# Four weight buffers shared across stages, odd Fourier weights made in place, and a Nyquist row summed by VectorE

## The chip, the core and the metric

The kernel runs on one core of one Trainium2 chip. The core has TensorE (PE in the profile) for matmuls, VectorE (DVE), ScalarE (ACT) and GpSimd (POOL) for the rest, and SyncE (SP), which here only issues transfers. Each engine takes its instructions in order and waits for others by semaphores. Transfers (DMAs) are issued by SP, ACT and POOL. The metric is the time of the whole program on the device in microseconds (us).

## The reference

Two layers of an encoder over 512 tokens with 1024 channels, in float32. Each layer is a half-step feed-forward network (FFN), a gated pair of mixers, and a second half-step FFN:

```python
x += 1/2 * SwiGLU(RMSNorm(x))                       # FFN 1, width 2816
x += W_o( g_na * NA(h) W_na + g_f * FNet(h) W_f )   # mixer, h = RMSNorm(x)
x += 1/2 * SwiGLU(RMSNorm(x))                       # FFN 2
...
s = einsum(q, k_window) * scale + bias              # neighbourhood attention, 8 heads
p = softmax(s);  o = einsum(p, v_window)
f = jnp.fft.fft2(ug, axes=(1, 3), norm="ortho").real   # Fourier mixer, 4 groups of 128
```

The gates g_na and g_f are sigmoids of `h @ w + gate_bias`. A last RMSNorm follows the second layer.

## The kernel before, in words

**Weights as a stream.** All weights lie in DRAM as granules of 128x1024 floats, 512 KB each. `stage_items` lists the granules in the order of their use, and `Stream` (`ws`) works through the list. `fetch` loads (L155, by SP) up to `depth` = `FETCH` = 8 items ahead of the one that is prepared next, and never beyond the current `stage`; `ws.enter(stage)` opens the next one. `prep` makes two tiles from a granule: `whi`, a rounded copy by ScalarE (L207, or L202 with the sign changed), and `wlo`, what the rounding lost, by VectorE (L210, L203). Three buffers of each exist. TensorE multiplies with both and with the rounded and lost parts of the activations: twelve matmuls of 512 columns for one granule (L534, L535, L537).

**Sums of weights.** The large products are done with seven products of half-size blocks in place of eight (Strassen's scheme), for which weights have to be added. Blocks are called a, b, c, d, and products m1 to m7. Where a tile needs the sum of two granules, either GpSimd issues a second transfer that adds in memory (L165 after the load, L212 after the granule has been used once), or VectorE adds two tiles (L179). In the first gate block, the products run in the order 1, 2, 5, 6, 7, 3, 4; m7 uses c (with a added by L165), m3 uses d with first a and then b added (L212).

**Buffers.** In an FFN stage the granules lie in nine buffers `raw` of the stage's own pool, which `swap_pools` opens and closes. In the mixer they lie in slots of a general pool (`slot`, 23 buffers), which also holds activations. The attention's bias tiles `bm` (one per head, 512 KB) have four buffers in the mixer's stage pool; `bias_for` loads two of them by SP.

**End of the mixer, start of the gates.** The order of DVE, ACT and PE is written out by hand here; SP and POOL are ordered by the scheduler. Attention probabilities of pairs 5, 6 and 7 are made (`maxes` on DVE with the bias tiles, L1433; exponentials on ACT; transposes and products on PE), in between the Fourier part. `part_f` multiplies with four Fourier weights. For each of the two column halves i there are two granules t1 and t2; the kernel uses t1 + t2 ("even") and t1 - t2 ("odd"). The even one is loaded with t2 added by GpSimd. For the odd one t1 is loaded a second time beside t2, and DVE subtracts (L179). `f_both` forms sum and difference in `fs` and `gs`, and `f_turn` copies rows of `gs` in mirrored places of `fs` by 8 small transfers for each i (L1681, "flips"). The Nyquist row (one frequency that stands alone) is the sum of three rows that `last_f` leaves on partitions 0, 32 and 64 of a PSUM bank; `f_last` copies the bank (L1686) and adds the rows by three tiny GpSimd transfers into row 3 of `fs` (L1691, L1693). `minus` makes the differences of activations for the gates' products in two steps (L1623). Then `gate_block` runs twice: at m7 the result of earlier products is copied out by ScalarE (`snap`, tile `sn`, L619) before TensorE writes to the same bank again.

Of the kernel before, what the change touches and what calls it, by code (L numbers as in the profile page):

```python
# [18 lines left out]
P = 128  # L19
# [15 lines left out]
FETCH = 8  # L35
# [63 lines left out]
def encoder_kernel(  # L99
# [8 lines left out]
    wp = ctx.enter_context(tc.tile_pool(name="wp", bufs=1))  # L108
    kp = ctx.enter_context(tc.tile_pool(name="kp", bufs=1))
# [9 lines left out]
    def slot(dt=F32, s="k", shape=(4, 256)):  # L119
        return kp.tile([P, *shape], dt, tag="k", name=nm(s), bufs=23)  # L120

# [23 lines left out]

    class Raw:
        def __init__(self, key, n=1024, plus=None):
            self.key, self.n, self.plus, self.t = key, n, plus, None

        def load(self, parts=1):  # L150
            if self.t is None:
                self.t = raw_pool[0](self.n)
                for c in range(0, self.n, self.n // parts):
                    cs = slice(c, c + self.n // parts)
                    nc.sync.dma_start(out=self.t[:, cs], in_=wst[GRAN_AT[self.key]][:, cs])  # L155
# [11 lines left out]
    class Item:  # L167
        def __init__(self, raw, add=None, neg=False, stage=0, parts=1, pieces=1, then=None, op=ALU.add):
            self.raw, self.add, self.neg, self.stage, self.parts, self.op = raw, add, neg, stage, parts, op
            self.pieces, self.then = pieces, then  # L170

# [5 lines left out]
        def summed(self):  # L177
            if self.add:
                V.tensor_tensor(self.raw.t, self.raw.t, self.add.t, self.op)  # L179
                self.add = None  # L180

        def prep_high(self):

            self.summed()
            n, t = self.raw.n, self.raw.t
            hi, lo = [wp.tile([P, 1024], F32R, tag=s, name=nm(s), bufs=3)[:, 0:n] for s in ("whi", "wlo")]
            S.activation(hi, t, AF.Copy)
            self.out = (hi, lo)

            def low():  # L190
                self.last = V.tensor_tensor(lo, t, hi.bitcast(F32), ALU.subtract)

            return low

        def prep(self, nxt):
# [8 lines left out]
            else:  # L204
                for c in range(0, n, n // self.parts):
                    cs = slice(c, c + n // self.parts)
                    S.activation(hi[:, cs], t[:, cs], AF.Copy)  # L207
                    if nxt:
                        nxt.summed()
                    self.last = V.tensor_tensor(lo[:, cs], t[:, cs], hi[:, cs].bitcast(F32), ALU.subtract)  # L210
            if self.then:
                G.dma_start(out=t, in_=wst[GRAN_AT[self.then]][:, 0:n], accum_op=ALU.add)  # L212
            self.out = (hi, lo)
# [3 lines left out]
    def stage_items():  # L217
# [52 lines left out]
        for l in range(L):  # L270
# [9 lines left out]
            for t1, t2 in halves:  # L280
                add(Raw(t1, plus=t2))
            for t1, t2 in halves:
                add(Raw(t1), Raw(t2), op=ALU.subtract)
# [840 lines left out]
    def stage_mixer(l, norm, nxt):  # L1124
# [94 lines left out]
        def proj_UV():  # L1219
# [31 lines left out]
            bias_for(0)  # L1251
# [4 lines left out]
            k0 = proj_T(None)  # L1256
            step(7)
# [94 lines left out]
        def four_high(ps, z):  # L1352
# [7 lines left out]
            def low_of():  # L1360
# [6 lines left out]
                V.tensor_copy(nyq[:, z, 0:1], ps[:, 256:257])  # L1367
# [4 lines left out]
        def four_ends(ps):  # L1372
# [7 lines left out]
            def low_of():  # L1380
                V.scalar_tensor_tensor(e_, g.bitcast(F32), ch[:, 162:163], t, ALU.mult, ALU.add)
                V.tensor_tensor(nyq[:, 2, 0:1], ps[:, 256:257], ch[:, 160:161], ALU.mult)
# [5 lines left out]
        def bias_for(hp):  # L1388
            bms[hp] = []
            for e in range(2):  # L1390
                res = mp.tile([P, 4, 256], F32, tag="bm", name=nm("bm"), bufs=4)
                nc.sync.dma_start(out=res, in_=bias_in[(l * NH + 2 * hp + e)])
# [290 lines left out]
        def f_last(i, ps):  # L1683

            t = tmp(s="fl")
            V.tensor_copy(t[0:96], ps[0:96])  # L1686
            to = fs[i, 0][3:4, 1, :]
            for z in range(3):
                row = t[32 * z : 32 * z + 1]
                if z == 0:  # L1690
                    G.dma_start(out=to, in_=row)  # L1691
                else:
                    G.dma_start(out=to, in_=row, accum_op=ALU.add)  # L1693

        with tc.manual_schedule(engines={mybir.EngineType.DVE, mybir.EngineType.Activation}):
            with tc.manual_schedule(engines={mybir.EngineType.PE}):
# [90 lines left out]
                p[5].maxes(1)  # L1787
                p[5].exps(0)
# [5 lines left out]
                pf = [part_f(0, t, f_w[0], 0) for t in range(2)]  # L1794
                att_split(po[0])
# [13 lines left out]
                att_split(po[1])  # L1809
                p[6].maxes(0)  # L1810
# [11 lines left out]
                pl = [last_f(i, raws[i]) for i in range(2)]  # L1822
                p[7].maxes(0)
                p[7].maxes(1)
                p[6].scaled(0)
# [5 lines left out]
                for i in range(2):  # L1831
                    f_last(i, pl[i])
# [3 lines left out]
                p[7].inverse(1)  # L1836
                p[7].scaled(0)
                p[7].scaled(1)
                first = minus(B[0, 0], B[0, 1], "t1")
                next(first)  # L1840
                next(first)
                pt_[6] = kept(ts)
                att_split(po[2])
                ws.enter(ws.stage + 1)
# [5 lines left out]
                swap_pools(0)  # L1850
# [141 lines left out]
    def swap_pools(kind, fetch=True):  # L1992
# [219 lines left out]
```

## Time and profile before

| | before |
|---|---|
| median of 3 runs | 1862.14 us (1859.94 to 1864.39) |
| profiled execution | 1860.03 us |
| its span | 1858.3 us |
| mean granted TensorE clock | 0.994 |
| read from memory, written | 372.76 MB, 2.11 MB |
| weight loads of 512 KB by SP, by GpSimd | 472, 180 |

The profile shows one execution. "Busy" is the time in which an engine worked; a timeline row has start, length, engine, line, operation, tiles (out<-in) and in brackets the idle time ahead of it with the one who ended it. "SPq" is SP's own queue of instructions, which issue transfers. The clock is a share of full speed. These two lines of the page show the clock and the transfers in 40 equal slices of the span (tenths, and GB/s):

```profile
PEclk9999999999999999999999999999999999999999
GB/s 304 223 242 213 187 280 285 205 199 85 283 217 183 167 229 241 215 198 279 249 190 214 226 224 202 282 251 226 160 124 273 214 181 177 219 232 215 200 286 157
```

The tenth and the thirtieth slices, with 85 and 124 GB/s, are the ends of the two mixers.

### The profile page before, as it was taken

To read this page: it belongs to the slowest core of one execution; us is meant where nothing else is said; L and a number is where in the kernel's file an instruction comes from. 1 tells how busy PE (TensorE), PEld (TensorE's weight loads), DVE (VectorE), ACT (ScalarE), POOL (GpSimd) and SP (SyncE) were. 2 spreads that over 40 slices of the span, in tenths; PEclk is the share of its full clock that TensorE was granted. 3 is DMA by queue.
4 is the path that set the end of the run, shared out by engine and by line. 5 is a ranking of instruction groups with operands and counts; after the bars stand their busy time and mean duration, and the time that the engine had idled before them with its cause. 6 is when DMAs were issued, how large, how long until landed. Compare 5 with 4: busy or idle time off the path is not lost.

```text
span 1858.3 us, 24537 instructions
## 1 busy us (share of the span) xinstructions
PE 1829.5 (98%) x8778; PEld 1514.2 (81%) x8778; DVE 1604.3 (86%) x1938; ACT 1306.1 (70%) x1775; POOL 187.7 (10%) x231
## 2 busy tenths in 40 slices
PE   9999999999899999999999999999998899999998
PEld 7888888887778888888888888888877788888886
DVE  7878899777889987889998888997788799888899
ACT  6777875677576777787667778666675677677865
POOL 0001010110111010001010100101011101110010
PEclk9999999999999999999999999999999999999999
DMA  9898799862987788869878986978539877888695
GB/s 304 223 242 213 187 280 285 205 199 85 283 217 183 167 229 241 215 198 279 249 190 214 226 224 202 282 251 226 160 124 273 214 181 177 219 232 215 200 286 157
DMA packets 206770, 405.87 MB, mean 218 GB/s; under 512 B 109116, under 2 KB 109276, under 8 KB 206648
## 3 DMA queue, kind: packets, MB, share of 16 engines
q1 hardware_dynamic: 176536, 302.61, 50.5%
q0 software_dynamic: 29680, 101.14, 29.9%
q8 instruction: 69, 1.13, 0.3%
q10 hardware_dynamic: 432, 0.55, 0.1%
q14 instruction: 53, 0.43, 0.1%
HBM read 372.76 MB, written 2.11 MB: 202 GB/s over the span
## 4 chain that ended last, share of the span: by engine, by line
PE 90%; DMA 4%; DVE 3%; ACT 2%; issue 1%; SPq 0%; ACTq 0%; DVEq 0%
PE A L534 10%; PE A L537 10%; PE A L535 10%; PE o L537 7%; PE o L534 7%; PE o L535 7%; PE B L534 5%; PE B L535 5%; PE B L537 5%; DMA raw<-in_wst_dram 2%; PE C L534 2%; PE C L535 2%; PE C L537 2%; PE ps L339 2%; PE ps L340 2%; PE ps L341 2%
## 5 line engine op out<-in xcount | busy, mean ns | idle before, releaser
L210 DVE TENSOR_TENSOR wlo<-raw,whi 128x1024 fp32r<-128x1024 f32 (+1 forms) x534 | 632.6, 1196 | 181.0 <-ACT whi L207 177.5
L207 ACT ACTIVATE whi<-raw 128x1024 fp32r<-128x1024 f32 (+1 forms) x534 | 546.7, 1033 | 292.4 <-PE A L535 60.4
L165 POOL DMA_DIRECT2D raw<-in_wst_dram x170 | 148.9, 895 | 1218.4 <-DMA raw<-in_wst_dram 636.3
L179 DVE TENSOR_TENSOR raw<-raw,raw 128x1024 f32<-128x1024 f32 (+1 forms) x152 | 181.6, 1197 | 2.0
L535 PE MATMUL A<-whi,xl 128*128 128x512 f32 x400 | 155.7, 389 | 0.0
L534 PE MATMUL A<-whi,xh 128*128 128x512 f32 x400 | 155.7, 389 | 0.0
L202 ACT ACTIVATE whi<-raw 128x1024 fp32r<-128x1024 f32 (+1 forms) x83 | 85.7, 1037 | 46.9 <-PE A L535 11.4
L389 ACT ACTIVATE at<-zt 128x1024 uint16<-128x1024 uint16 (+2 forms) x96 | 110.3, 1166 | 11.3 <-DMA zt<-zs 11.3
L537 PE MATMUL A<-wlo,xh 128*128 128x512 f32 x400 | 115.0, 389 | 0.0
L203 DVE SCALAR_TENSOR_TENSOR wlo<-raw,whi 128x1024 fp32r<-128x1024 f32 (+1 forms) x83 | 98.8, 1198 | 12.3 <-ACT whi L202 12.3
L537 PEld LDWEIGHTS A<-wlo,xh 128*128 128x128 f32 x400 | 75.1, 188 | 15.6
L534 PEld LDWEIGHTS A<-whi,xh 128*128 128x128 f32 x400 | 75.1, 188 | 15.4
L535 PEld LDWEIGHTS A<-whi,xl 128*128 128x128 f32 x400 | 75.1, 188 | 15.4
L534 PE MATMUL B<-whi,xh 128*128 128x512 f32 x208 | 81.2, 390 | 0.0
L535 PE MATMUL B<-whi,xl 128*128 128x512 f32 x208 | 81.0, 389 | 0.0
L535 PE MATMUL C<-whi,xl 128*128 128x512 f32 x208 | 81.0, 389 | 0.0
L534 PE MATMUL C<-whi,xh 128*128 128x512 f32 x208 | 80.9, 389 | 0.0
L370 ACT ACTIVATE zs<-th 128x1024 uint16<-128x1024 uint16 x80 | 79.4, 1040 | 0.4 <-DVE th L794 0.4
L787 ACT ACTIVATE th<-sn,rh 128x512 f32<-128x512 f32 x80 | 54.8, 715 | 31.2 <-DVE sn L624 30.3
L619 ACT ACTIVATE sn<-A 128x512 f32<-128x512 f32 x104 | 58.4, 584 | 22.9 <-PE A L537 22.9
L537 PE MATMUL C<-wlo,xh 128*128 128x512 f32 x208 | 59.8, 389 | 0.0
L537 PE MATMUL B<-wlo,xh 128*128 128x512 f32 x208 | 59.8, 389 | 0.0
(446 smaller groups left out, 4641.4 us busy)
## 6 DMA issues: line engine op xcount, KB each, us to landing
raw<-in_wst_dram SPq DMA_DIRECT2D x472, 512.0 KB, 6.0
raw<-in_wst_dram POOLq DMA_DIRECT2D x180, 512.0 KB, 8.1
bm<-in_bias_dram SPq DMA_DIRECT2D x16, 512.0 KB, 5.9
raw<-in_wst_dram SPq DMA_DIRECT2D x30, 256.0 KB, 5.9
vs<-v SPq DMA_DIRECT2D x24, 128.0 KB, 5.6
x<-in_xin_dram SPq DMA_DIRECT2D x4, 512.0 KB, 10.2
raw<-in_wst_dram POOLq DMA_DIRECT2D x8, 256.0 KB, 7.4
dft<-in_dft_dram POOLq DMA_DIRECT2D x8, 256.0 KB, 6.7
```

What stands on the lines that cost most here:

```text
L165: G.dma_start(out=self.t, in_=wst[GRAN_AT[self.plus]][:, 0 : self.n], accum_op=ALU.add)
L179: V.tensor_tensor(self.raw.t, self.raw.t, self.add.t, self.op)
L202: S.activation(hi, t, AF.Copy, scale=-1.0)
L203: self.last = V.scalar_tensor_tensor(lo, t, -1.0, hi.bitcast(F32), ALU.mult, ALU.subtract)
L207: S.activation(hi[:, cs], t[:, cs], AF.Copy)
L210: self.last = V.tensor_tensor(lo[:, cs], t[:, cs], hi[:, cs].bitcast(F32), ALU.subtract)
L370: S.activation(s[:, h], words[:, h], AF.Copy)
L389: S.activation(to[:, w], t[:, w], AF.Copy)
L534: PE.matmul(ps, lh, rh, start=start, stop=False, skip_group_check=again)
L535: PE.matmul(ps, ll, rh, start=False, stop=False, skip_group_check=again)
L537: PE.matmul(ps, lh, rl, start=False, stop=stop, skip_group_check=again)
L619: S.activation(t[:, b, :], ps[b], AF.Copy)
```

## The change

1. A pool `rp` with four buffers `kr` lives through the whole program. They hold the attention's bias tiles in the mixer, then the first four granules of the gates (`mix_raw`), and FFN granules. The FFN stage's own `raw` buffers go from nine to five; `ffn_raw` takes, of all nine, the one whose last use is the oldest.
2. At the end of the mixer the stream enters the gates' stage earlier, with a depth of 6, so that the gates' first granules may be loaded there. The depth goes back to 8 afterwards.
3. The odd Fourier weight is made in the buffer of the even one: (t1 + t2) - 2 t2, by one scalar_tensor_tensor of DVE. t1 is not loaded again.
4. The Nyquist row is summed by DVE: one copy of 32x512 out of PSUM and two additions; the column that carries it is number 3, so that it comes out on the right row. `last_f(0)` runs earlier, and `f_last(0)` and `f_last(1)` stand in two places.
5. `minus` for the first difference, and the first bias load (now issued by ACT), move.

```diff
+    rp = ctx.enter_context(tc.tile_pool(name="rp", bufs=1, reuse_waits="tile"))
...
+    def kept_raw(s, shape=(1024,)):
+        return rp.tile([P, *shape], F32, tag="kr", name=nm(s), bufs=4)
...
             self.key, self.n, self.plus, self.t = key, n, plus, None
+            self.refs = self.used = 0
+
+        def use(self):
+            uses[0] += 1
+            self.refs, self.used = self.refs - 1, uses[0]
...
-                self.t = raw_pool[0](self.n)
+                self.t = raw_pool[0](self)
...
+        def __init__(self, raw, add=None, neg=False, stage=0, parts=1, pieces=1, then=None, twice=False):
+            self.raw, self.add, self.neg, self.stage, self.parts, self.twice = raw, add, neg, stage, parts, twice
             self.pieces, self.then = pieces, then
+            raw.refs += 1
+            if add:
+                add.refs += 1
...
         def summed(self):
             if self.add:
-                V.tensor_tensor(self.raw.t, self.raw.t, self.add.t, self.op)
+                if self.twice:
+                    V.scalar_tensor_tensor(self.raw.t, self.add.t, -2.0, self.raw.t, ALU.mult, ALU.add)
+                else:
+                    V.tensor_tensor(self.raw.t, self.raw.t, self.add.t, ALU.add)
+                self.add.use()
                 self.add = None
...
-                    if nxt:
+                    if nxt and not nxt.twice:
                         nxt.summed()
...
+            self.raw.use()
...
             halves = [((s, "f", 2 * i), (s, "f", 2 * i + 1)) for i in range(2)]
-            for t1, t2 in halves:
-                add(Raw(t1, plus=t2))
-            for t1, t2 in halves:
-                add(Raw(t1), Raw(t2), op=ALU.subtract)
+            even = [Raw(t1, plus=t2) for t1, t2 in halves]
+            for raw in even:
+                add(raw)
+            for raw, (_, t2) in zip(even, halves):
+                add(raw, Raw(t2), twice=True)
...
-            bias_for(0)
...
             k0 = proj_T(None)
+            bias_for(0, S)
...
-                V.tensor_copy(nyq[:, z, 0:1], ps[:, 256:257])
...
-                V.tensor_tensor(nyq[:, 2, 0:1], ps[:, 256:257], ch[:, 160:161], ALU.mult)
+                V.tensor_tensor(nyq[:, 2, 3:4], ps[:, 256:257], ch[:, 160:161], ALU.mult)
...
-        def bias_for(hp):
+        def bias_for(hp, by=nc.sync):
             bms[hp] = []
             for e in range(2):
-                res = mp.tile([P, 4, 256], F32, tag="bm", name=nm("bm"), bufs=4)
-                nc.sync.dma_start(out=res, in_=bias_in[(l * NH + 2 * hp + e)])
+                res = kept_raw("bm", (4, 256))
+                by.dma_start(out=res, in_=bias_in[(l * NH + 2 * hp + e)])
                 bms[hp].append(res)
...
         def f_last(i, ps):
 
-            t = tmp(s="fl")
-            V.tensor_copy(t[0:96], ps[0:96])
-            to = fs[i, 0][3:4, 1, :]
-            for z in range(3):
-                row = t[32 * z : 32 * z + 1]
-                if z == 0:
-                    G.dma_start(out=to, in_=row)
-                else:
-                    G.dma_start(out=to, in_=row, accum_op=ALU.add)
+            to = fs[i, 0][0:32, 1, :]
+            V.tensor_copy(to, ps[0:32])
+            for z in (1, 2):
+                V.tensor_tensor(to, to, ps[32 * z : 32 * z + 32], ALU.add)
...
                 p[5].maxes(1)
+                first = minus(B[0, 0], B[0, 1], "t1")
+                next(first)
+                next(first)
...
                 pf = [part_f(0, t, f_w[0], 0) for t in range(2)]
+                pl = [last_f(0, raws[0])]
...
                 att_split(po[1])
+                f_last(0, pl[0])
                 p[6].maxes(0)
...
                 pf = [part_f(0, t, f_w[1], 1) for t in range(2)]
-                pl = [last_f(i, raws[i]) for i in range(2)]
+                pl.append(last_f(1, raws[1]))
+                ws.enter(ws.stage + 1)
                 p[7].maxes(0)
                 p[7].maxes(1)
+                ws.items[ws.prepped].summed()
+                ws.depth = 6
+                ws.enter(ws.stage + 1)
...
                 f_copy(1, 0, pf[0])
                 f_copy(1, 1, pf[1])
-                for i in range(2):
-                    f_last(i, pl[i])
                 po.append(att_pv(2))
                 ts = transposed(p[6].s)
                 p[7].inverse(0)
                 p[7].inverse(1)
+                ws.prep(ws.pos + 2)
+                f_last(1, pl[1])
                 p[7].scaled(0)
                 p[7].scaled(1)
...
-                first = minus(B[0, 0], B[0, 1], "t1")
-                next(first)
-                next(first)
                 pt_[6] = kept(ts)
                 att_split(po[2])
-                ws.enter(ws.stage + 1)
                 ws.prep(ws.pos + 2)
                 f_w.append(ws.next(0))
                 f_both(0, 0, part_f(1, 0, f_w[2]))
...
                 ts = transposed(p[7].s)
-                swap_pools(0)
+                swap_pools(0, False)
+                ws.depth = FETCH
+                ws.enter(ws.stage)
...
-    def ffn_raw(n):
-        return scope_pool[0].tile([P, 1024], F32, tag="raw", name=nm("raw"), bufs=9)[:, 0:n]
-
-    def mix_raw(n):
+    live = {"kr": [None] * 4, "raw": [None] * 5}
+
+    def oldest(tag):
+
+        ages = [0 if r is None else (r.used if not r.refs else 1 << 30) for r in live[tag]]
+        k = min(range(len(ages)), key=lambda i: ages[i])
+        return ages[k], tag, k
+
+    def ffn_raw(raw):
+        _, tag, k = min(oldest("kr"), oldest("raw"))
+        live[tag][k] = raw
+        if tag == "kr":
+            return kept_raw("raw")[:, 0 : raw.n]
+        return scope_pool[0].tile([P, 1024], F32, tag="raw", name=nm("raw"), bufs=5)[:, 0 : raw.n]
+
+    def mix_raw(raw):
+        if raw.key[1] in ("ga", "gb") and None in live["kr"]:
+            live["kr"][live["kr"].index(None)] = raw
+            return kept_raw("raw")
         return slot(F32, "raw", (1024,))
...
             raw_pool[0] = mix_raw
+            live["kr"] = [None] * 4
         else:
             raw_pool[0] = ffn_raw
+            live["raw"] = [None] * 5
```

What the change moves, by the built programs' order. SP's queue at the end of the first layer's mixer, before: two loads `raw` (the n granules), three flips, then the six loads for a, b and d.

```order
L1211 DMA vs_724_3716<-v_709_3660 64x512 x4
L155 DMA raw_811_4166<-in_wst_dram 128x1024
L155 DMA raw_812_4168<-in_wst_dram 128x1024
L1681 DMA fs_773_3978<-gs_816_4181 60x512 x2
L1681 DMA fs_772_3976<-gs_816_4181 60x512
L155 DMA raw_821_4207<-in_wst_dram 128x1024
L155 DMA raw_822_4209<-in_wst_dram 128x1024
```

The same place in the change (raw_802 and raw_803 are a0 and a1, raw_800 and raw_801 the n granules, raw_804 and raw_820 b, raw_821 and raw_822 d):

```order
L166 DMA raw_802_4111<-in_wst_dram 128x1024
L166 DMA raw_803_4113<-in_wst_dram 128x1024
L166 DMA raw_800_4102<-in_wst_dram 128x1024
L166 DMA raw_801_4104<-in_wst_dram 128x1024
L166 DMA raw_804_4115<-in_wst_dram 128x1024
L166 DMA raw_820_4208<-in_wst_dram 128x1024
L166 DMA raw_821_4210<-in_wst_dram 128x1024
L166 DMA raw_822_4213<-in_wst_dram 128x1024
L1702 DMA fs_774_3985<-gs_815_4182 60x512 x2
L1702 DMA fs_773_3983<-gs_815_4182 60x512 x2
```

All loads now stand ahead of all flips. SP's queue at the end of the flips, before (gb: the gate biases; raw_855 and raw_858: c0 and c1):

```order
L1681 DMA fs_801_4111<-gs_835_4263 4x512 x2
L1681 DMA fs_800_4109<-gs_835_4263 3x512
L1892 DMA gb_851_4369<-in_gbias_dram 128x1024
L1892 DMA gb_852_4371<-in_gbias_dram 128x1024
L155 DMA raw_855_4375<-in_wst_dram 128x1024
L155 DMA raw_858_4382<-in_wst_dram 128x1024
```

and in the change (raw_851 and raw_854 are c0 and c1):

```order
L1702 DMA fs_806_4127<-gs_831_4258 4x512 x2
L1702 DMA fs_805_4125<-gs_831_4258 3x512
L166 DMA raw_851_4370<-in_wst_dram 128x1024
L166 DMA raw_854_4377<-in_wst_dram 128x1024
L166 DMA raw_866_4438<-in_wst_dram 128x1024
L1915 DMA gb_847_4364<-in_gbias_dram 128x1024
L1915 DMA gb_848_4366<-in_gbias_dram 128x1024
```

c0 and c1 have gone ahead of the gate biases. VectorE behind the last maxima (L1433, L1454), before: the Fourier copies, the two copies for the Nyquist rows, and the two differences.

```order
L1668 COPY fs_4109<-ps_4071 128x512
L1668 COPY fs_4111<-ps_4080 128x512
L1686 COPY fl_4113<-ps_4089 96x512
L1686 COPY fl_4118<-ps_4093 96x512
L1445 RECIPROCAL rs_4068<-sm_4067 128x2 x2
L1623 TENSOR_TENSOR t_807_4156<-xh_2214 128x1024
L1623 TENSOR_TENSOR t_808_4157<-xl_2215 128x1024
L1494 TENSOR_TENSOR o_4163<-ps_4123,o_4163 128x512
L210 TENSOR_TENSOR wlo_4171<-raw_3464,whi_4170 128x1024
```

and in the change:

```order
L194 SCALAR_TENSOR_TENSOR raw_3382<-raw_3465,raw_3382 128x1024
L1689 COPY fs_4125<-ps_4080 128x512
L1689 COPY fs_4127<-ps_4089 128x512
L1466 RECIPROCAL rs_4077<-sm_4076 128x2 x2
L229 TENSOR_TENSOR wlo_4159<-raw_3382,whi_4158 128x1024
L1707 COPY fs_4125<-ps_4098 32x512
L1709 TENSOR_TENSOR fs_4125<-fs_4125,ps_4098 32x512 x2
L1515 TENSOR_TENSOR o_4172<-ps_4129,o_4172 128x512
```

The odd weight's subtraction has come here, the differences have gone to an earlier place, and three small instructions stand for one copy (the other three stand ahead of the sixth maxima). SP's queue in the first block of the second layer's first FFN, in the change (loads are numbered in the order of the list):

```order
L166 DMA raw_1579_8224<-in_wst_dram 128x1024
L166 DMA raw_1585_8250<-in_wst_dram 128x1024
L166 DMA raw_1595_8306<-in_wst_dram 128x1024
L166 DMA raw_1604_8350<-in_wst_dram 128x1024
L166 DMA raw_1626_8479<-in_wst_dram 128x1024
L166 DMA raw_1592_8286<-in_wst_dram 128x1024
L166 DMA raw_1640_8562<-in_wst_dram 128x1024
```

Before, all loads of this stretch stood in the order of the list; now raw_1592, the third granule of c, stands behind three that are used after it. It is the granule whose buffer, counted in weight preparations along the engines' orders, is released three preparations ahead of its own; in the first block of the FFNs ahead of and behind this one (the second of each layer) it is five. Before the change it was eight or more for every granule that is added to.

More of the change, by code (lines that the diff above doesn't have):

```diff
@@ L143, in encoder_kernel @@
         PE.matmul(pw, warm[:, 0:P], warm, start=True, stop=True)
+    uses = [0]
     class Raw:
@@ L167, in encoder_kernel @@
     class Item:
-        def __init__(self, raw, add=None, neg=False, stage=0, parts=1, pieces=1, then=None, op=ALU.add):
-            self.raw, self.add, self.neg, self.stage, self.parts, self.op = raw, add, neg, stage, parts, op
+        def __init__(self, raw, add=None, neg=False, stage=0, parts=1, pieces=1, then=None, twice=False):
+            self.raw, self.add, self.neg, self.stage, self.parts, self.twice = raw, add, neg, stage, parts, twice
             self.pieces, self.then = pieces, then
+            raw.refs += 1
+            if add:
+                add.refs += 1
         def load(self):
@@ L212, in prep @@
                 G.dma_start(out=t, in_=wst[GRAN_AT[self.then]][:, 0:n], accum_op=ALU.add)
+            self.raw.use()
             self.out = (hi, lo)
@@ L1366, in low_of @@
                 V.memset(y[:, 2:4, 0:1].bitcast(F32), 0.0)
-                V.tensor_copy(nyq[:, z, 0:1], ps[:, 256:257])
+                V.tensor_copy(nyq[:, z, 3:4], ps[:, 256:257])
                 return y
```

## The prediction

> **What bounds the kernel now.** I read the page first, then the waits of TensorE, then the rows of TensorE around its waits, then the chain of work that ends in the longest of them.
>
> ```profile
> PE 1829.5 (98%) x8778; PEld 1514.2 (81%) x8778; DVE 1604.3 (86%) x1938; ACT 1306.1 (70%) x1775; POOL 187.7 (10%) x231
> engine line waited for: us in total, times, longest us
> PE A L534 <- ACT sn L619: 19.1, 4, 6.1
> PE ps L143 <- DVE ones L139: 1.2, 1, 1.2
> PE ps L340 <- DVE wlo L210: 0.4, 2, 0.2
> ```
>
> TensorE is busy for 1829.5 of 1858.3 us. Nothing that leaves its work alone can win more than the 28.8 us in which it is idle and whatever it loses to a lower clock. Two thirds of the idle time, 19.1 us, are four waits of one kind. All stand at product 7 of the gate blocks, two in each layer.
>
> ```profile
> 496.73 0.79 PE L534 MATMUL A<-whi,t3h 128*128 128x512 f32 x1 [6.13 <-ACT sn L619]
> 502.04 0.39 PE L534 MATMUL A<-whi,t3h 128*128 128x512 f32 x1
> 541.17 0.50 PE L534 MATMUL A<-whi,t3h 128*128 128x512 f32 x1 [2.67 <-ACT sn L619]
> 1417.03 0.79 PE L534 MATMUL A<-whi,t3h 128*128 128x512 f32 x1 [5.59 <-ACT sn L619]
> 1420.35 0.39 PE L535 MATMUL A<-whi,t3l 128*128 128x512 f32 x1
> 1462.63 0.80 PE L534 MATMUL A<-whi,t3h 128*128 128x512 f32 x1 [4.69 <-ACT sn L619]
> 1468.40 0.39 PE L534 MATMUL A<-whi,t3h 128*128 128x512 f32 x1
> 1468.62 0.39 PE L535 MATMUL A<-whi,t3l 128*128 128x512 f32 x1
> ```
>
> In brackets stands the wait and who ended it. At full clock these matmuls start 0.227 us apart (1468.40 to 1468.62, rounded), and one granule of weights feeds twelve, 2.72 us. After the wait of 6.13 us twelve matmuls take 502.04 - 496.73 = 5.31 us, so the slow clock costs 2.59 us more. After 5.59 us seven take 3.32 us in place of 1.59, which is 1.73 us more. After 2.67 us nothing is lost behind the wait. The first block's waits thus cost 6.13 + 2.59 + 5.59 + 1.73 = **16.0 us** in both layers. The second block's (2.67, and 4.69 with its ramp) are some 10 us, and have another cause, below.
>
> The chain of waits into 496.73 (start, us, what) says what the first kind is:
>
> ```profile
> 469.45 6.68 DMA fs<-gs
> ...
> 476.15 7.03 DMA raw<-in_wst_dram
> ...
> 483.46 11.57 DMA raw<-in_wst_dram
> ...
> 496.10 0.59 ACT sn L619
> ```
>
> The second granule c1 of product 7 is loaded at 476.15, its other half added by a GpSimd transfer at 483.46, which lands at 495.03. ScalarE, in order, converts it and then takes the snapshot `sn` that TensorE waits for. From landing to matmul it is 1.70 us. The load is late for its place in SP's in-order queue:
>
> ```profile
> 444.03 0.80 SPq L155 DMA_DIRECT2D raw<-in_wst_dram  x2
> 453.64 2.79 SPq L1681 DMA_DIRECT2D fs<-gs  x3
> 456.53 3.86 SPq L155 DMA_DIRECT2D raw<-in_wst_dram  x6
> 460.43 13.61 SPq L1681 DMA_DIRECT2D fs<-gs  x13
> 474.14 0.83 SPq L1892 DMA_DIRECT2D gb<-in_gbias_dram  x2
> 475.02 22.78 SPq L155 DMA_DIRECT2D raw<-in_wst_dram  x9
> ```
>
> Six weight loads, sixteen flips of the Fourier result and two gate biases stand ahead of it. The windows (stretch, length, busy PE, PEld, DVE, ACT, POOL, granted clock, DMA share, GB/s) show the contrast:
>
> ```profile
> 420.00:428.00 8.00, 8.00 (x49) 6.26 (x49) 4.70 (x21) 5.53 (x14) 0.00 (x0) 1.00 0.00 0
> 436.00:444.00 8.00, 8.00 (x76) 6.57 (x72) 7.05 (x19) 6.00 (x16) 0.00 (x0) 1.00 0.01 2
> 472.00:488.00 16.00, 16.00 (x73) 13.24 (x72) 15.46 (x16) 7.46 (x10) 3.28 (x4) 1.00 1.02 320
> 488.00:504.00 16.00, 9.87 (x33) 7.41 (x32) 8.53 (x8) 7.09 (x8) 1.90 (x3) 0.79 1.05 264
> ```
>
> The transfers rest until 444 and are full from 472 to 504.
>
> **The change part by part.** *Early gate weights.* The first four granules a0, a1, b0, b1 go into kept buffers. SP's new order has them ahead of the flips, and c0, c1 ahead of the gate biases; the last bias buffers are released by the score maxima. a0 and a1 fall into the empty stretch before 444. Ahead of c1 the queue no longer has the 3.86 us of six loads between flips and the 0.83 us of two biases: 4.7 us. With every transfer as long as before, c1 lands at 495.03 - 4.7 = 490.3, and TensorE starts at 492.0. It is due at 496.73 - 6.13 = 490.6, so 1.4 us of wait are left. If the accumulate takes less time in the emptier queues, nothing is left:
>
> ```profile
> raw<-in_wst_dram SPq DMA_DIRECT2D x472, 512.0 KB, 6.0
> raw<-in_wst_dram POOLq DMA_DIRECT2D x180, 512.0 KB, 8.1
> ```
>
> Its median is 8.1 us against the 11.57 here. What is late next is product 3, whose granules are added to by L212 while product 7 runs:
>
> ```profile
> L212 POOL DMA_DIRECT2D raw<-in_wst_dram x2: 863/863/863, 485.5 to 487.3; - x2
> ...
> DMA to landing us min/median/max: 12.1/13.1/14.0
> ```
>
> They land at 485.5 + 12.1 = 497.6 and 487.3 + 14.0 = 501.3. Without the wait TensorE ends product 7 at 490.6 + 24 x 0.227 = 496.05. With 1.1 us of conversion (the whi group's mean is 1.03) the first is ready at 498.7, 2.7 us late. The second, ready at 502.4, is due at 498.7 + 2.7 = 501.4, 1.0 late. So with unchanged transfers 3.7 us come back per layer, and with a median transfer of 8.1 us (landing at 493.6 and 495.4) none. Between 0 and 3.7 I take 1.5 us, next to the sum for c1 at old durations; waits under 2.67 us cost no clock. Two layers: **-16.0 + 3.0 us**.
>
> *Odd Fourier weights and the Nyquist row.* Two 512 KB loads a layer go. The subtraction on VectorE becomes a scalar_tensor_tensor of the same shape. The group means 1197 and 1198 ns say that this costs nothing:
>
> ```profile
> L179 DVE TENSOR_TENSOR raw<-raw,raw 128x1024 f32<-128x1024 f32 (+1 forms) x152 | 181.6, 1197 | 2.0
> L203 DVE SCALAR_TENSOR_TENSOR wlo<-raw,whi 128x1024 fp32r<-128x1024 f32 (+1 forms) x83 | 98.8, 1198 | 12.3 <-ACT whi L202 12.3
> 445.93 1.28 DVE L1686 COPY fl<-ps 96x512 f32<-96x512 f32 x2
> 447.89 1.21 DVE L1623 TENSOR_TENSOR t<-xh 128x1024 f32<-128x1024 f32 x1
> 452.94 0.68 DVE L1675 TENSOR_TENSOR gs<-fs,ps 128x512 f32<-128x512 f32 x1
> 453.07 0.50 PE L340 MATMUL ps<-wlo,y 128*128 128x512 f32 x1 [0.20 <-DVE wlo L210]
> ```
>
> The Nyquist row was two copies (1.28 us together) and six tiny DMAs per layer. It becomes two copies of 32x512 and four additions, which no row shows. They have 512 columns, like the copy at 0.64 and the sum from PSUM at 0.68 us; I take 0.64, six times, 3.8 us, which is 2.6 more. If fewer partitions were faster it would be less, down to nothing. Three of the six (1.9 us) stand ahead of the sixth maxima, from which one weight subtraction (1.2 us) goes, so these come 0.7 us later. The two differences of L1623 (1.21 us each) leave the stretch 447 to 450 for one where DVE is busy for 4.70 of 8 us. The wait of 0.20 us at 453.07 shows that TensorE has no reserve there, so 0.7 us come through, at most the 1.9 of three operations. I take 1.0 us a layer: **+2.0 us**. The tiny DMAs waited beside GpSimd's other work and paid nothing.
>
> *The four shared buffers in the FFN.* Nine buffers become four kept and five of the stage, chosen by the oldest use. The transfers stay as many, the order of loads on SP changes. TensorE does not wait in any FFN before. I take 0; the bound is a rival below. *First attention bias* issued by ScalarE behind a snapshot near 350 us, while the first maxima stand at 372.6 and a bias lands in about 6: 0.
>
> *Second gate block.* Its waits end with the same snapshot, but there the chain comes from a transpose:
>
> ```profile
> 529.80 9.51 DMA zt<-zs
> ...
> 539.34 0.03 ACT mq L389
> ```
>
> ScalarE, in order, stands before the words `mq` that it unpacks until the transpose lands, and the snapshot is behind it. No part of the change touches what starts this transpose, and the transfers beside it stay, so I take 0; bounds are the whole 10 us and, the other way, one 5 us load that now meets it.
>
> Sum: -16.0 + 3.0 + 2.0 = **-11.0 us**. The profiled execution took 1860.0 us (span 1858.3), so it would be 1849.0. The median of the three runs, 1862.1, lies 2.1 above the profiled one; the forecast is 1851.
>
> **The rivals.** *The wait moves to product 3.* The accumulates are no faster than before, and 3.7 us return per layer: -16.0 + 7.4 + 2.0 = -6.6, **1855.5**. For it speaks the DMA share of 1.02 and 1.05; against it, that c's accumulates end before L212's begin to need the engines.
>
> By the Trainium skill, "DMA: Bandwidth & Descriptors", section "Queues, rings and completion order", each transfer engine goes round the queues that have work, packet by packet, so GpSimd's accumulate gets its turn and no more as long as one SP load is queued; that favours this case. The trace has 12.1 us beside a full SP queue and 8.1 in the median, which agrees with it only in direction.
>
> *The FFN starves.* This is the case on the slower side. In the first block of three FFN stages the third granule of c takes a buffer released shortly before. The new order gives it three weight preparations in one stage and five in two, where the old gave eight or more. A load and its accumulate take 6.0 + 8.1 = 14.1 us, conversion 2.2; three preparations are 8.2 us, five 13.6. The shortfalls are 8.1 + 2.7 + 2.7 = 13.5, and 2.6 for the clock after the long one: -11.0 + 16.1 = +5.1, **1867**. It decides from 11 us of such waits on. Against it: weights are converted into three buffers, which is up to 5.4 us of reserve.
>
> *The loads do not come early.* If c1 still lands near 495, because the flips stretch over the time the loads left or the early loads wait for their buffers, only the additions remain: **1864**.
>
> *The second block gains too*: up to -10 more, **1842**.
>
> **How the numbers follow.** Chances: the forecast 0.42, product 3 0.20, starving 0.17, no early loads 0.13, second block 0.08. The range leaves out the farther parts of the last and of starving: 1841 to 1867. A difference of 0.2%, 3.7 us, is about what a measurement can tell from none. Faster: 0.42 + 0.20 + 0.08, less 0.04 for a thin margin of the second case, 0.66. Slower: 0.17. Same: 0.17.
>
> **What would show it.** Right: no wait over 2.7 us at the first block's product 7, c1 loaded by about 471, no matmuls at 0.43 us spacing there, a0 and a1 issued before 444, the FFN without waits. Wrong: a wait of TensorE at product 3 on L207's successor, waits for `raw` in the first block of an FFN, transposed probabilities late near 450, or c1 still issued after 475.

## The result, and the profile after

The changed kernel takes 1875.18 us (median of 4 runs, 1874.41 to 1880.74) against 1861.04 us for the kernel before in the same runs. The ratio is 1.0081, with a 95% interval of 1.0056 to 1.0106: the change makes the kernel 14 us slower. The forecast was 1851, the range ended at 1867.

From the page of the changed kernel, its span and the busy time of each engine:

```profile
span 1873.8 us, 24519 instructions
PE 1835.4 (98%) x8778; PEld 1516.7 (81%) x8778; DVE 1608.8 (86%) x1946; ACT 1304.7 (70%) x1775; POOL 178.9 (10%) x219
```

The waits of TensorE in the same kernel (who waited, for whom, us in total, times, longest):

```profile
PE A L555 <- ACT sn L640: 10.0, 4, 3.6
PE A L555 <- ACT whi L226: 8.2, 1, 8.2
PE hA L623 <- ACT whi L226: 5.0, 2, 2.7
PE ps L1438 <- ACT q L1193: 2.0, 2, 1.5
PE ps L1438 <- DVE q L1200: 1.5, 2, 0.7
```

The four waits for the snapshot `sn` have shrunk from 19.1 to 10.0 us in total, so that part came. Beneath them stand waits that were not there before: 8.2 and 5.0 us for a converted weight `whi`, and 3.5 us in the attention (`q`). TensorE's busy time has grown by 5.9 us with the same 8778 matmuls: part of them ran slowly.

Both kernels run 8778 matmuls, so one can ask by how much the same matmul starts later in the profile after. I paired them in their order and took the difference of the starts in the two traces, each stretch ending where the matmuls behind it run at full rate again:

| stretch (time in the profile before) | lateness at its end, us | added |
|---|---|---|
| FFN 1, layer 1 (to 310) | 1.3 | +1.3 |
| first attention products (366 to 369) | 2.9 | +1.6 |
| rest of the mixer, to the gates (to 469) | 4.3 | +1.4 |
| gates and what follows (to 649) | 0.1 | -4.2 |
| FFN 2, layer 1: wait and slow matmuls (649 to 656) | 4.5 | +4.4 |
| FFN 1, layer 2: wait and slow matmuls (962 to 966) | 15.6 | +11.1 |
| first attention products (1287 to 1290) | 19.8 | +4.1 |
| rest of the mixer (to 1390) | 21.1 | +1.3 |
| gates and what follows (to 1573) | 11.7 | -9.4 |
| FFN 2, layer 2: wait and slow matmuls (1573 to 1577) | 15.8 | +4.1 |

The gates win 13.6 us. The three places of waits and slow matmuls in the FFNs lose 19.6, the first attention products 5.7, the end of the mixer 2.7, and FFN 1 of the first layer 1.3, around a wait of 0.7 us for VectorE near 308. The spans differ by 15.5.

The largest loss in TensorE's timeline of the changed kernel:

```profile
975.77 0.80 PE L555 MATMUL A<-whi,t7h 128*128 128x512 f32 x1 [8.24 <-ACT whi L226]
976.36 0.63 PE L556 MATMUL A<-whi,t7l 128*128 128x512 f32 x1
...
981.06 0.42 PE L623 MATMUL hC<-xh,whi 128*128 128x256 f32 x1
```

After a wait of 8.24 us the twelve matmuls of one granule take 981.06 - 975.77 = 5.29 us in place of 2.72. The chain of waits into it (start, us, what):

```profile
954.89 1.26 DVE wlo L229
956.15 0.02 issue
956.16 10.64 DMA raw<-in_wst_dram
966.80 0.02 issue
...
967.38 7.18 DMA raw<-in_wst_dram
...
974.66 1.06 ACT whi L226
```

Read from the end: the conversion waits for the accumulate (7.18 us), this for the load (10.64 us), and the load for VectorE to finish with the tile that had the buffer. The load could not begin earlier, because its **buffer came free late**. The two transfers were also longer than their medians in the profile before (10.64 + 7.18 us against 6.0 + 8.1), which makes 3.7 of the 8.24 us. That is the starving rival, at product 7 of the first block, in the three FFN stages that it named. The waits are 2.67, 8.24 and 2.31 us, 13.2 together; the rival's sum of shortfalls was 13.5.

In the gates the chain of the changed kernel ends so:

```profile
490.39 7.72 DMA raw<-in_wst_dram
498.21 1.06 ACT whi L226
499.27 0.49 ACT sn L640
499.81 0.51 PE A L555
```

Here it is no longer c1 that is waited for. The transfer issued at 490.39 adds b to d for product 3. Its conversion stands in ScalarE's order ahead of the second half of the snapshot, and product 7 needs the snapshot.

### The profile page after: what moved, and what is told of

Same layout as the page of the kernel before. It is cut to its first block, busy times and chain, and to the rows that moved or that the text cites. A ratio compares the mean times of both kernels' runs of the same rounds, so it can differ in the third digit from the quotient of the medians.

```text
span 1873.8 us, 24519 instructions
## 1 busy us (share of the span) xinstructions
PE 1835.4 (98%) x8778; PEld 1516.7 (81%) x8778; DVE 1608.8 (86%) x1946; ACT 1304.7 (70%) x1775; POOL 178.9 (10%) x219
## 4 chain that ended last, share of the span: by engine, by line
PE 55%; DMA 9%; DVE 8%; issue 5%; ACT 3%; SPq 1%; POOL 0%; DVEq 0%; POOLq 0%; ACTq 0%
DMA raw<-in_wst_dram 8%; PE A L555 6%; PE A L558 6%; PE A L556 6%; PE o L555 4%; PE o L556 4%; PE o L558 4%; PE B L555 3%; PE B L556 3%; PE B L558 3%; DVE wlo L229 2%; PE ps L360 2%; PE ps L361 2%; PE ps L362 2%; PE C L556 1%
## 5 line engine op out<-in xcount | busy, mean ns | idle before, releaser
L196 DVE TENSOR_TENSOR raw<-raw,raw 128x1024 f32<-128x1024 f32 (+1 forms) x148 | 176.8, 1195 | 4.0 <-DMA raw<-in_wst_dram 2.0
L555 PEld LDWEIGHTS A<-whi,xh 128*128 128x128 f32 x400 | 75.1, 188 | 15.5
L558 PEld LDWEIGHTS A<-wlo,xh 128*128 128x128 f32 x400 | 75.1, 188 | 15.5
L555 PE MATMUL A<-whi,t7h 128*128 128x512 f32 x136 | 54.1, 398 | 8.2 <-ACT whi L226 8.2
```

The source lines that it names most:

```text
L196: V.tensor_tensor(self.raw.t, self.raw.t, self.add.t, ALU.add)
L555: PE.matmul(ps, lh, rh, start=start, stop=False, skip_group_check=again)
L558: PE.matmul(ps, lh, rl, start=False, stop=stop, skip_group_check=again)
```

## The experiments

**1. The rule for buffers that are all in use.** When `ffn_raw` is called and all nine buffers still have a reader to come, the change's rule gives each the same age, and the minimum falls on the kept ones. The experiment orders them by their last planned use.

```diff
+            ends[0] += 1
+            raw.end = ends[0]
+            if add:
+                add.end = ends[0]
...
-        ages = [0 if r is None else (r.used if not r.refs else 1 << 30) for r in live[tag]]
+        ages = [0 if r is None else (r.used if not r.refs else (1 << 30) + r.end) for r in live[tag]]
```

> The change with one thing altered: where all nine FFN buffers are still in use, ffn_raw takes the one whose last planned use comes first, not the first of the kept ones. Theory A (the rule for busy buffers starves the FFN): the waits of 2.67, 8.24 and 2.31 us before product 7 of the first block of three FFN stages go, with the slow matmuls behind them, 18 to 19 us together, so about 1856 us against 1875. Theory B (the four buffers are late because bias tiles and gate weights use them too, or the pool is split in two): the waits stay whatever the rule, about 1875 us.

Measured: 1861.85 us (12 runs), ratio 0.9998 (0.9987 to 1.0009). The three waits are gone. The windows over the three places (stretch, length, busy PE, PEld, DVE, ACT, POOL, granted clock, DMA share, GB/s), first of the changed kernel, then of the experiment:

```profile
640.00:664.00 24.00, 21.33 (x117) 18.95 (x117) 17.70 (x22) 8.23 (x10) 2.28 (x4) 0.93 0.82 246
960.00:984.00 24.00, 15.76 (x70) 12.97 (x69) 11.20 (x12) 6.38 (x8) 1.67 (x3) 0.79 0.59 156
1580.00:1600.00 20.00, 17.69 (x104) 16.06 (x103) 13.87 (x17) 6.34 (x8) 1.71 (x2) 0.91 0.81 241
```

```profile
640.00:664.00 24.00, 24.00 (x142) 21.31 (x141) 21.87 (x25) 12.15 (x14) 2.31 (x3) 1.00 0.95 222
950.00:974.00 24.00, 24.00 (x141) 21.33 (x141) 19.03 (x21) 14.05 (x17) 2.62 (x4) 1.00 0.75 171
1570.00:1590.00 20.00, 20.00 (x124) 18.01 (x123) 18.92 (x23) 10.03 (x11) 2.31 (x3) 1.00 0.93 272
```

TensorE is busy throughout and the clock is full. Theory A holds in its mechanism. Of its 18 to 19 us some 15 came by the two ratios (1.0081 and 0.9998, each against the kernel before in the same runs), 13.3 by the medians. The rest is not explained wholly: in this profile, taken from a run of 1865.9 us, 3 us are lost in small pieces in the FFNs' output products of the middle of the program and 3 more in the last FFN, without a wait over 0.7 us.

**2. The same rule in the kernel before.** All nine buffers stay in the stage's own pool, under two tags of four and five; nothing is shared with the mixer.

```diff
-    def ffn_raw(n):
-        return scope_pool[0].tile([P, 1024], F32, tag="raw", name=nm("raw"), bufs=9)[:, 0:n]
+    def ffn_raw(raw):
+        _, tag, k = min(oldest("kr"), oldest("raw"))
+        live[tag][k] = raw
+        n = 4 if tag == "kr" else 5
+        return scope_pool[0].tile([P, 1024], F32, tag=tag, name=nm("raw"), bufs=n)[:, 0 : raw.n]
```

> The kernel before with one part of the change alone: its nine FFN buffers, all of the stage's own pool, split into four and five and chosen by the change's rule. Nothing is shared with the mixer. Theory A: the same three waits appear, 13 us and some 5 us of slow matmuls, about 1879 us against 1861. Theory B (sharing is the cause): no waits, about 1861 us.

Measured: 1883.6 us (6 runs), ratio 1.0124 (1.0097 to 1.0151). TensorE's waits:

```profile
PE A L547 <- ACT sn L632: 32.7, 4, 19.0
PE A L547 <- ACT whi L219: 8.0, 1, 8.0
PE hA L615 <- ACT whi L219: 6.2, 2, 3.2
```

The three waits are here, 8.0 and 6.2 us, as in the changed kernel. The rule alone makes them, without sharing. (One wait of 19.0 us in the second gate block belongs to this profiled run, the slowest of its six; it stands in no other profile and I don't explain it.)

**3. The bias tiles back at their place.** On top of experiment 1, `bias_for(0)` is issued by SP where it was.

```diff
+            bias_for(0)
             q0 = proj_T(DH**-0.5)
...
-            bias_for(0, S)
```

> As planned_rule, and the first two attention bias tiles are again loaded by SP at the place of before. Theory A2 (the later bias loads delay the accumulating transfers ahead of the first attention products): the waits of 0.55 and 0.75 us at 368 us and of 1.49 and 0.75 at 1305 us go, and with them 1.8 us per layer and the 0.9 us behind, about 4 us less than planned_rule, 1852 us. Theory B2 (ScalarE's order or issue is the cause): the waits stay and the time is that of planned_rule.

Measured: 1858.8 us, ratio 0.9978 (0.9962 to 0.9993), against 0.9998 for experiment 1; the intervals overlap. In the first layer the waits at 368 us went, but 2.2 us of new ones came between 334 and 343 us. In the second layer the old ones stayed and 1.9 us of new ones came. SP, in order, now stands at the bias loads until a kept buffer is free, with weight loads behind. Neither theory held as stated.

**4. Without the early entry into the gates.** On top of experiment 1:

```diff
-                ws.depth = 6
-                ws.enter(ws.stage + 1)
...
-                swap_pools(0, False)
-                ws.depth = FETCH
-                ws.enter(ws.stage)
+                swap_pools(0)
...
-        if raw.key[1] in ("ga", "gb") and None in live["kr"]:
-            live["kr"][live["kr"].index(None)] = raw
-            return kept_raw("raw")
```

> As planned_rule, without the early gate weights: these lie in mixer slots again and are loaded after the attention as before. Theory A3 (the early loads alone shorten the waits of the gates): the waits at product 7 return to about 6 us in the first block of both layers, with the slow clock, so 8 to 13 us more than planned_rule, 1864 to 1869 us. Theory B3 (c ahead of the gate biases, or two loads fewer, does it): the waits stay near 3.5 us and the time within 2 us of planned_rule.

Measured: 1859.36 us, ratio 0.9982 (0.9969 to 0.9995). The experiment missed what it meant to test: the granules still get kept buffers, by way of `ffn_raw`, and the scheduler moves the loads to the same place in SP's queue. The interval overlaps that of experiment 1, so no effect of these lines on the time can be told. The kernel serves as the base of what follows.

**5. SP's queue held as before.** The six loads for a, b and d are traced behind flips, which also puts the gate biases ahead of c0 and c1.

```diff
-                swap_pools(0)
+                flips = f_turn(0)
+                with tc.issue_after(flips[2].ins):
+                    swap_pools(0)
```

> As planned_late_gates (which turned out to issue the gate loads as early as the change does), but the six loads for a, b and d are held behind five flips, and the gate biases stand ahead of c0 and c1: SP's order of before, all other parts of the change kept. Theory A3 (the order of SP's queue is what shortened the gates' waits): the waits at product 7 return to 5 to 6 us with slow matmuls behind them, 5 to 8 us more than planned_late_gates in all, 1864 to 1867 us. Theory B3 (two loads fewer and the lighter GpSimd did it): waits near 3.4 and 2.5 us as in planned_late_gates, 1859 us.

Measured: 1875.8 us, ratio 1.0073 (1.0056 to 1.0089), 16 us more than its base. SP's queue in its timeline:

```profile
443.27 0.81 SPq L166 DMA_DIRECT2D raw<-in_wst_dram  x2
461.23 6.32 SPq L1707 DMA_DIRECT2D fs<-gs  x8
467.60 3.10 SPq L166 DMA_DIRECT2D raw<-in_wst_dram  x6
```

And of TensorE's waits in it:

```profile
PE A L559 <- ACT sn L644: 7.4, 3, 3.6
PE B L559 <- ACT whi L230: 5.3, 2, 2.9
```

Neither theory held as stated. The time rose, so the order of SP's queue matters. But the waits of theory A3, 5 to 6 us at product 7 of the first blocks, did not return: they are 3.6 and 3.2 us there, as in the base (3.4 and 2.5). The loss stands at product 5 (`B`) and around it. And the order is not the one of before: all eight flips of the first half stand ahead of the loads, not three, so that a loads at 467.6, where before it stood at 456.5. So it is not shown how much of the gates' win comes from the order.

**6. The snapshot ahead of the conversion.** On top of experiment 4:

```diff
                         s2 = snap(pa)
+                        ws.prep(ws.pos + 3)
                         with_n(arg(s1, 0, 0), 0)
```

> As planned_late_gates, and ScalarE copies out both halves of the snapshot behind product 6 before it converts the next granule (d with b added). Theory A4 (the wait at product 7 is only ScalarE's order: the second half of the snapshot stands behind a conversion that waits for the accumulate of L231): the waits of 3.4 and 2.5 us in the first blocks go with the slow matmuls behind them, 8 us in all, 1851 us; product 3 does not wait. Theory B4 (the accumulate is late for product 3 itself): the same wait appears at product 3, 1859 us.

Measured: 1860.01 us, ratio 0.9989 (0.9976 to 1.0002), no gain over its base. The first blocks' waits at product 7 did go; new ones of 1.83 us stand at product 4, where TensorE waits for VectorE (`xl`, L371).

**7. The first bias tiles earlier, from ScalarE.** On top of experiment 4:

```diff
             step(5)
+            bias_for(0, S)
             def t1():
...
-            bias_for(0, S)
```

> As planned_late_gates, and the first two bias tiles are issued by ScalarE ahead of the first product of the mixer, some 25 us earlier. Theory A2 (the bias transfers meet the accumulates ahead of the first attention products): the waits of 1.2 to 2.0 and 0.75 us at 368 and 1293 us go, 2 to 3 us per layer, 1854 us. Theory B2: they stay, 1859 us.

Measured: 1863.01 us, ratio 0.9992 (0.9976 to 1.0008). The waits at 368 us went in the first layer; as in experiment 3, others came at 335 and 342 us. The second pair's load, which stays with SP, now stands in SP's queue ahead of weight loads.

**8. The Nyquist row as before, first try.** `f_last`, `last_f` and `minus` as in the kernel before, on top of experiment 4. Here the first row's matmuls read the weights after the subtraction in place, so the Nyquist row holds other values; the work is the same.

```diff
-                pl = [last_f(0, raws[0])]
...
-                f_last(0, pl[0])
...
-                pl.append(last_f(1, raws[1]))
+                pl = [last_f(i, raws[i]) for i in range(2)]
```

> As planned_late_gates, with the Nyquist row again copied by VectorE and summed by tiny GpSimd transfers, its matmuls and the differences of activations at their places of before. Theory A5 (the six small instructions and the later maxima cost 1.5 us per layer at the end of the mixer): 3 us less, 1856 us, and the wait of 0.57 us at 446 us goes. Theory B5 (the odd weights in place delay the maxima): the time stays at 1859 us.

Measured: 1859.57 us, ratio 0.9982 (0.9969 to 0.9995): as its base. In the profile the wait of 0.57 us at 446 us is gone and the mixer's end is 1.6 us shorter in the first layer and 1.8 in the second, but the time does not show it.

**9. Four bias tiles into the gap.** On top of experiment 4, both pairs are issued by ScalarE behind its squares.

```diff
-                norm.squares(1, 0)
+                with tc.issue_after(norm.squares(1, 0).ins):
+                    bias_for(0, S)
+                    bias_for(1, S)
...
-            bias_for(0, S)
...
-                bias_for(1)
```

> As planned_late_gates, with the first four bias tiles (first and second pair) issued by ScalarE behind its squares near 331 us, where the transfers rest (DMA share 0.02 at 332 to 336). In early_bias two of them had stood in SP's queue ahead of weight loads and the wait had only moved to 341 us. Theory A2 (bias transfers that meet the accumulates delay the first attention products): no waits over 0.3 us between 330 and 375 us nor at the same place of the second layer, 3 us less per layer than planned_late_gates, 1854 us. Theory B2: the waits at 368 us stay, 1859 us.

Measured: 1851.77 us (6 runs), ratio 0.9942 (0.9920 to 0.9964), **the fastest of all**, 8.9 us less than the kernel before; its interval lies below that of its base. Its five largest waits:

```profile
PE A L560 <- ACT sn L645: 9.1, 4, 3.6
PE ps L147 <- DVE ones L143: 1.2, 1, 1.2
PE ps L364 <- DVE o L1521: 1.1, 2, 0.6
PE ps L365 <- DVE wlo L233: 0.9, 1, 0.9
PE ps L1444 <- DVE q L1205: 0.6, 1, 0.6
```

Of the 4.6 us that the base waited for `q` 0.6 are left, in the second layer. Theory A2 holds, and its cause shows in the changed kernel's chain into the attention:

```profile
349.35 15.48 DMA raw<-in_wst_dram
364.83 0.02 issue
...
364.94 1.07 ACT whi L226
```

The accumulate takes 15.48 us with the bias transfers of 351.8 beside it. The same one took 10.9 us in the kernel before and takes 12.5 here. In the stretch from 332 to 336 us, where the bias transfers now run, the DMA share is 0.97, and TensorE is busy throughout.

**10. The second block's snapshot too.**

```diff
-            joined_words(mq[0, j], turned[j])
+            with tc.issue_after(snap.last.ins):
+                joined_words(mq[0, j], turned[j])
```

> As snap_first, and in the second gate block ScalarE unpacks the transposed words behind the second half of the snapshot too. Theory A4: the waits of 2.3 and 2.9 us at the second blocks' product 7 go as well, no wait over 1 us there; 3 to 5 us less than snap_first in the gates, 1855 us. Theory B4: they come back at product 3 or 4, 1860 us.

Measured: 1862.83 us, ratio 0.9996 (0.9972 to 1.0021). No wait for `sn` is left in the profile, and nothing is won. Waits of 3.3 us for `xl` at product 4 of the first blocks and 3.8 us for `wlo` (L365) are there instead, as theory B4 has it in kind.

**11. The Nyquist row as before, second try.** As 8, with the first row's matmuls kept early:

```diff
-                pl = [last_f(i, raws[i]) for i in range(2)]
+                pl.append(last_f(1, raws[1]))
```

> As planned_late_gates, with the Nyquist row copied by VectorE and summed by tiny GpSimd transfers as before, and the differences of activations at their place of before; unlike in old_nyquist the matmuls of the first row stay ahead of the subtraction in place. Theory A5 (the six small instructions cost 1.5 us a layer): 3 us less, 1856 us. Theory B5: 1859 us.

Measured: 1859.83 us, ratio 0.9991 (0.9978 to 1.0004). No difference from its base (0.9982) can be told: theory A5's 3 us are not confirmed in the time. In the profile the mixer's end is 1.0 and 1.5 us shorter in the two layers than in the base.

**12. All three together.**

> bias_gap, snap_both and nyquist_ok together. If the three gains are real and independent (3 us per layer, 3 to 4 us per layer in the gates, 1.5 us per layer), 1845 us. If TensorE meets the next late transfer each time, 1853 to 1858 us.

Measured: 1853.19 us, ratio 0.9950 (0.9931 to 0.9968), no better than experiment 9. Where the snapshots' 9.1 us went shows in the windows, first of experiment 9, then of this kernel:

```profile
488.00:504.00 16.00, 12.38 (x48) 9.77 (x47) 11.69 (x12) 7.69 (x9) 3.42 (x4) 0.89 1.05 296
504.00:520.00 16.00, 16.00 (x72) 13.26 (x71) 14.97 (x18) 9.55 (x11) 1.72 (x2) 1.00 0.75 183
```

```profile
488.00:504.00 16.00, 14.87 (x62) 10.87 (x61) 10.45 (x12) 8.19 (x10) 2.59 (x3) 1.00 1.06 295
504.00:520.00 16.00, 14.17 (x61) 11.35 (x62) 16.00 (x18) 9.49 (x11) 1.73 (x2) 1.00 0.71 171
```

And of its waits:

```profile
PE ps L365 <- DVE wlo L233: 3.7, 2, 1.9
PE A L561 <- DVE xl L371: 3.7, 2, 1.8
```

TensorE arrives earlier at 504, but there VectorE is busy for all of the 16 us, and TensorE waits for it until the block ends. What was won at product 7 is given back at product 4 and behind the block.

## Why the prediction was wrong

- **What bounds the kernel** was read rightly: TensorE, with the gates' waits as the only large idle time.
- **Gates, -13.0 us.** They gave 13.6, but not as worked out, and that the totals agree is luck. The first blocks gave 7.4 (3.5 and 3.9), the second blocks and what follows 6.2, where I had 0; why these won is not shown. c1 was in time: it landed at 491.4, the sum had 490.3. But its load was issued at 474.6 and not at 471.5, and TensorE, 4.3 us late by then, reached product 7 at 494.7. I had the deadline of the next transfer wrong: d with b added is due not at product 3, but ahead of the snapshot's second half, because its conversion stands between the halves in ScalarE's order. So it was due at 499.81 - 3.57 = 496.2, less 1.7 for conversion and copy, 494.5, and landed at 498.1, although it took 7.72 us and not 12.1. That was the price of the rival "the wait moves to product 3" (3.7 us; measured 3.57 and 3.28 in the two layers), reached by another way, with a slow clock on top.
- **Early loads.** a0 was issued at 434.8, ahead of 444 as forecast. The early place comes from the kept buffers and the scheduler; for the lines that enter the gates early no effect can be told (experiment 4). That the queue's order matters for the time is shown (experiment 5), not how much of the gates' win it makes, nor how that would be shared by the early a and by c ahead of the biases.
- **End of the mixer, +2.0 us.** Lateness grew by 1.4 and 1.3, 2.7. With the Nyquist part and the differences of activations as before, this stretch is 1.0 to 1.8 us shorter in each layer in the profiles of experiments 8 and 11, near the 1.0 that I took, but the time does not show the gain.
- **"The four shared buffers in the FFN ... I take 0."** This is the step that failed. That TensorE waits in no FFN before was no reason for 0, as the new rule can put a load on a buffer that comes free late. It cost 19.6 us in the profile, 13.2 of waits, the rest slow matmuls behind them. The mechanism, the three places and the waits' sum were written down as a rival at 0.17, with up to 5.4 us of reserve from the three converted buffers held against it. Experiments 1 and 2 show that the rule for busy buffers does it, whether the buffers are shared or not. That the rival's shortfalls of 8.1, 2.7 and 2.7 became waits of 8.24, 2.67 and 2.31 is luck in part. From the release of the buffer to the time at which TensorE was ready for the granule there were 11.4, 15.1 and 15.1 us, where the rival counted 8.2 and 13.6: a reserve of 3.2 and 1.5 us was there. But from the release to the first matmul it took 19.6, 17.7 and 17.4 us and not 16.3, which used it up.
- **"First attention bias ... 0."** The second failure, 5.7 us. I checked that the bias itself lands in time (I took 6 us; its two transfers took 10.3 and 15.0) and not what they do to the accumulates around them.
- The rival's total, 1867, was 8 us low: it lacked the bias's 5.7 us, and the slow matmuls behind the three waits cost 6.4 us, where it had 2.6. The second block's rival comes to 1841 by its own sum, not 1842.

## What to carry to other kernels

When a rule chooses among buffers, ask what it does when all are in use: a tie broken by position can choose the one that is released last, and a load queued on it is late however early it stands in the program. Count the lead of each load, from the release of its buffer to its first use, before and after a change; where the lead is shorter than load and accumulate, expect a wait. A reserve held against it can go into transfers that are longer than their median, as it did here. Before a transfer is moved, see what it will share the engines with, and before a wait is removed, see which engine is full right behind it.

## What the runs showed of the hardware

The clock drops after shorter waits than the profile before suggested, from which the prediction took that waits under 2.67 us cost no clock. A wait of 2.67 us at 541.17 in the kernel before cost nothing behind it (granted clock 1.00 from 540 to 550). One of the same length at 652.32 in the changed kernel did (clock 0.83 from 650 to 660), as did one of 2.31 us (clock 0.79 from 1586 to 1594) and one of 3.57 us:

```profile
500.00:504.00 4.00, 4.00 (x11) 3.12 (x11) 3.79 (x4) 1.76 (x2) 0.85 (x1) 0.57 1.04 288
650.00:660.00 10.00, 7.68 (x38) 7.08 (x39) 7.71 (x10) 4.66 (x6) 0.00 (x0) 0.83 0.71 197
```

So the length of a wait alone doesn't tell. The Trainium skill, "TensorE: Matmul & The Clock Gate", section "What's actually happening", says that the clock falls back after at least one idle window of some 3.4 us, and that this window runs freely. By that rule a wait of 2.67 us, shorter than the window, would cost nothing; at 652.32 it did, and the measurement decides. No run here varied the place of a wait alone, so what tells the two apart stays open.
